# Hybrid attention encoder layer on one core: one stream of projections ahead of the attention, a shared bank for short scores, and values at odd blocks

## The chip, the cores and the metric

The kernel runs on one core of one Trainium2 chip. The metric is the device time of a run in microseconds. Engines are named TensorE (PE in the rows), VectorE (DVE), ScalarE (ACT), GpSimd (POOL) and SyncE (SP, used only to issue DMAs).

## What is computed

One encoder layer on two batches that share weights: a prompt of 1024 tokens and a sample of 512, width 1024, all in float32. Cut from the reference:

```python
hn = rms_norm(x, g_attn)
proj = hn @ w_in
qa, ka, va, qd, kd, vd = jnp.split(proj, 6, axis=-1)
oa = neighbourhood_attention(heads(qa), heads(ka), heads(va), rpb)   # 8 heads, 8 x 16 window, learned bias
od = dilated_attention(heads(qd), heads(kd), heads(vd), slopes)      # 8 heads, 3 patterns, merged by denominators
mix = jnp.concatenate([rms_norm(oa, g_na), rms_norm(od, g_dil)], axis=-1)
x = x + mix @ w_out
hn = rms_norm(x, g_ffn)
x = x + (jax.nn.silu(hn @ w_gate) * (hn @ w_up)) @ w_down
y = rms_norm(x, g_final)
```

## The kernel before

Every float32 operand of a product is split into a high and a low part, and a product is three matmuls: high by high, high by low, low by high (`mm3`, L155). Scores take two matmuls, since q holds its high part in 64 partitions and its low part in the other 64, and k's low parts stand in tiles of their own, `klow`.

**Pairs and blocks.** The 16 heads are taken two at a time, as 16 "pairs" (head pair times batch): pairs 0 to 7 of the prompt (R), 8 to 15 of the sample (S), each time dilated ("b") and neighbourhood ("a") in turn, so even pairs are dilated. A pair has 2 heads by 8 query blocks = 16 blocks in the prompt, and 8 blocks in the sample. A block goes through

- `scores`: two matmuls (L698 with k's high, L699 with k's low part) for each stretch of keys. A dilated prompt block has two stretches, a long one of 512 columns (`sc`) and a short one of 256 (`sc2`); other blocks have one;
- `softmax`: VectorE adds the bias table and takes the minimum, reading the scores' bank and writing `t` and `mt` (L739), ScalarE takes the exponential (L746);
- `turn`: transposes of `t` on TensorE (L756; 6 in a dilated prompt block, 3 in a neighbourhood one), eviction into `pT`, high part by ScalarE (L760), low part by VectorE (L761);
- `values`: matmuls of two blocks with V into one half of the bank `pv` (L776), then `head_out` on VectorE and GpSimd.

**Projections beside them.** While the blocks of pair i run, the q, k and v projections of pair i+1 are issued (`qkv`): three weight slices (v, q, k in this order) by one or two chunks of 512 tokens, in steps of six matmuls (L155, `acc<-hth,whi` and its two companions), 24 steps = 144 matmuls for a prompt pair and 72 for a sample pair. `Dense` spreads the steps evenly: block j may have consumed the share (j + 0.8)/n before its softmax and (j + 1)/n after it. After a projection's matmuls follow: for k the copies to `ka` (ScalarE) and the subtractions to `klow` (VectorE, `low(0)` and `low(1)`, L508), for v a scale, `vT` to fp16 high and low (dilated: `v16`; neighbourhood: `va`, in two halves, `v_high_a`) and transposing DMAs into `vnb` or `vna`. `after(n, f)` puts f behind n steps. Of chunk 0 of k, `low(1)` is held back (`held`) until the second-last block of the pair that runs, since `klow[1]` is a single tile that this pair's scores still read.

**What sets the order.** The engines' instruction order is made by a list scheduler from the order in which the program is written, from tile buffers and dependencies; the program's order is the priority. The opening (pair 0's projections, `opening`, with its scaling of x into hth and htl, L291 and L294) is ordered by hand on TensorE, VectorE and ScalarE. PSUM has eight banks: `mm` 2 (projections), `sc` 3 (scores), `pv` 1, `tp` 2 (transposes). Tags with their buffers in SBUF: `t` 3, `pT` 3, `p16` 3 (v16, va, dgs, bias_e), `ka` 3, `qa` 4, `tabb` 2.

**Bias tables.** `bias_load` loads the neighbourhood's relative bias into three tiles `bias_e` (nine DMAs each on SyncE, L325 and L329). `bias_rows` subtracts on VectorE (L334), writes to `e_d` in DRAM (L336), overwrites borders by GpSimd memsets (L337, L338), and writes `e2_d` (L339). It is written after pair 0's projections.

**Later phases.** After the pairs come the output projection (its first four tiles still beside pair 15) and the feed-forward (from about 830 us on), which the change doesn't touch.

Of the kernel before, what the change touches and what calls it, by code (L numbers as in the profile page):

```python
# [18 lines left out]
P = 128  # L19
# [15 lines left out]
DF = 0.8  # L35
# [3 lines left out]
TB, P16, PTB, OB = 3, 3, 3, 2  # L39
BANKS = dict(mm=("mm", 2), sc=("sc", 3), pv=("pv", 1), tp=("tp", 2))  # L40
# [16 lines left out]
def hymba_layer_kernel(  # L57
# [105 lines left out]
    def after(n, fn):  # L163
        agenda.append([n, fn])
# [8 lines left out]
    def flush():  # L173
        while agenda:
            agenda.pop(0)[1]()

    def run(gen):
        for _ in gen:
            tick()
# [37 lines left out]
    klow = [rb.tile([P, TP + 256], F32R, tag=f"kl{i}", name=f"kl{i}", bufs=1) for i in range(2)]  # L217
    held = []
# [103 lines left out]
    def bias_load():  # L322
        for t in range(3):
            f = rb.tile([P, NA + 1, 32], F32, tag="p16", name="bias_e", bufs=P16)
            nc.sync.dma_start(out=f[:, NA], in_=colm_d[t])  # L325
            for h in range(8):
                src = bass.AP(tensor=rpbf.tensor, offset=PAD + h * RPB - 4 * 31 + (-16, -8, 0)[t],
                              ap=[[1, 16], [31, NA], [1, 32]])
                nc.sync.dma_start(out=f[h * 16:(h + 1) * 16, :NA], in_=src)  # L329
            yield f  # L330
# [41 lines left out]
    def qkv(pi):  # L372
# [87 lines left out]
        def v_high_a(half):  # L460
# [10 lines left out]
            def low():  # L471
# [7 lines left out]
                if half == 0:  # L479
                    v_high_a(1)  # L480
                else:
                    v_undo()
# [11 lines left out]
        def k_put(ch, acc):  # L494
            if ch == 0:
# [5 lines left out]
                res["kl"] = [z[:, :nx] for z in klow]  # L501
# [11 lines left out]


            after(2, lambda: low(0))
            if pi and ch == 0 and st.nch == 2:
                held.append(lambda: low(1))
            else:
                after(2, lambda: low(1))
# [165 lines left out]
    def scores(k):  # L685
# [15 lines left out]
        if g == "b":  # L701
# [6 lines left out]
            if st.nch == 2:  # L708
                a, e = (1 - rr) * 512 + n * P, T + rr * P
                sc = bank("sc", "sc2")  # L710
# [188 lines left out]
    class Dense:  # L899
        def __init__(self, gen, total):  # L900
            self.gen, self.total, self.spent = gen, total, 0

        def upto(self, share):
            while self.gen is not None and self.spent < share * self.total:
                if next(self.gen, "end") == "end":
                    self.gen = None
                tick()
                self.spent += 1

        def rest(self):  # L910
            if self.gen is not None:
                run(self.gen)
            flush()

    pipe, owed = [], []

    def interleave(pi, dense):
        blocks = blocks_of(pi)
        n = len(blocks)
        tables(blocks[0])  # L920
        scores(blocks[0])
        for j, k in enumerate(blocks):
            if j + 1 < n:
                scores(blocks[j + 1])
            while j == n - 2 and held:
                held.pop()()
            dense.upto((j + DF) / n)
            softmax(k)
            pipe.append(k)
            while owed:  # L930
                head_out(owed.pop())
            if j % 2 == 0 and len(pipe) > LAG:
                values(pipe[:2])
                owed.append(pipe[1])
                del pipe[:2]
            if len(pipe) > 1:
                turn(pipe[-2])
            if j + TL < n:
                tables(blocks[j + TL])
            dense.upto((j + 1) / n)  # L940
        dense.rest()
# [4 lines left out]
    for pi in range(len(pairs)):  # L946
        if pi + 1 < len(pairs):
            dense = Dense(qkv(pi + 1), 12 * pairs[pi + 1][0].nch)
        else:
            dense = Dense(out_first(), 11 + 8 * NO)  # L950
        interleave(pi, dense)
# [505 lines left out]
```

## Time and profile before

| | us |
|---|---|
| runs | 1977.22, 1970.92, 1977.09 (median 1977.09) |
| profiled execution, its own time | 1966.33 |
| its span | 1964.3 |
| TensorE busy | 1842.0 (94%) |
| VectorE busy | 1321.1 (67%) |
| ScalarE busy | 916.4 (47%) |
| GpSimd busy | 844.1 (43%) |
| mean granted TensorE clock | 0.977 |

The rows that follow the change are of four kinds. A row of stretches gives for a window of the span the busy time of each engine with its count of instructions, the granted TensorE clock (1.00 is 2.4 GHz, the upper of its two levels; 0.5 is 1.2 GHz), and the share and rate of the DMA engines. A row of a timeline is a run of equal instructions: start, duration, engine, line, operation, tiles; in brackets the time that the engine idled before it and what ended the idling. A row of waits groups such idle time by what waited and what it waited for: total, times, longest. Rows of one line list what its instructions waited for.

### The profile page before, as it was taken

The numbers are of one execution on the slowest core, as the hardware profiler recorded it, in microseconds if no ns is written. First come the engines' busy times: TensorE is split into PE (matmuls) and PEld (weight loads), VectorE is DVE, ScalarE is ACT, GpSimd is POOL, SyncE is SP. The second block draws the span as 40 slices with busy tenths as digits, with TensorE's granted clock in tenths as the row PEclk, the third lists the DMA queues.
The fourth block names the chain that finished last, engine by engine and source line by source line (L and its number), as shares of the span: only waits on it lengthen the run. The fifth ranks groups of instructions, "written<-read, shape, count | busy, mean of one in ns | idle before, by whom it ended". The sixth has DMA issues, their size and how long they took to land.

```text
span 1964.3 us, 28970 instructions
## 1 busy us (share of the span) xinstructions
PE 1842.0 (94%) x10450; PEld 1609.9 (82%) x10450; DVE 1321.1 (67%) x2626; ACT 916.4 (47%) x1731; POOL 844.1 (43%) x690
## 2 busy tenths in 40 slices
PE   6889999898999998999899999879999997999998
PEld 4777777677777776788899999879999995877886
DVE  7566656656656567566976777877767665757765
ACT  5455557555566667443433333433333332324431
POOL 4323324232355551100666666656666543642110
PEclk9999999999899998999999999989999998999999
DMA  7623323232344455353354343334343448866642
GB/s 263 142 66 99 88 82 104 58 88 69 97 108 119 117 164 143 136 161 118 107 150 130 108 131 101 113 109 122 105 131 104 132 127 314 272 217 234 226 166 94
DMA packets 218943, 265.97 MB, mean 135 GB/s; under 512 B 59584, under 2 KB 163152, under 8 KB 218800
## 3 DMA queue, kind: packets, MB, share of 16 engines
q1 hardware_dynamic: 196176, 179.57, 30.4%
q0 software_dynamic: 22624, 84.56, 14.5%
q8 instruction: 82, 1.34, 0.3%
q14 instruction: 61, 0.50, 0.1%
HBM read 202.71 MB, written 51.41 MB: 129 GB/s over the span
## 4 chain that ended last, share of the span: by engine, by line
PE 74%; DVE 9%; DMA 7%; issue 4%; ACT 3%; POOL 2%; SPq 0%; DVEq 0%; POOLq 0%; ACTq 0%
PE acc L155 37%; PE yacc L155 11%; PE zacc L155 7%; PE mmacc L155 7%; PE pt L756 4%; PE pv L776 3%; PE sc L698 2%; DVE flo L1080 2%; PE sc L699 2%; DMA left<-hid_d 1%; DMA fraw<-in_w_up_dram 1%; POOL fs L1084 1%; DVE t L739 1%; PE pt L210 1%; DMA wq<-in_w_down_dram 1%
## 5 line engine op out<-in xcount | busy, mean ns | idle before, releaser
L155 PE MATMUL acc<-dhi,left 128*128 128x512 f32 x924 | 289.8, 394 | 16.6 <-ACT left L1254 14.0
L155 PE MATMUL acc<-hth,whi 128*128 128x512 f32 x576 | 233.5, 405 | 7.1 <-DVE kl L508 5.4
L155 PE MATMUL acc<-htl,whi 128*128 128x512 f32 x576 | 231.3, 401 | 1.0 <-POOL htl L294 0.5
L1080 DVE TENSOR_TENSOR flo<-fs,fhi 128x512 fp32r<-128x512 f32 x176 | 173.8, 991 | 86.2 <-ACT fhi L1079 85.1
L155 PE MATMUL acc<-hth,wlo 128*128 128x512 f32 x576 | 230.5, 400 | 0.1
L155 PEld LDWEIGHTS acc<-dhi,left 128*128 128x128 f32 x924 | 174.1, 189 | 57.8 <-ACT left L1254 15.3
L1079 ACT ACTIVATE fhi<-fs 128x512 fp32r<-128x512 f32 x176 | 109.5, 629 | 188.3 <-POOL fs L1084 81.4
L125 POOL TENSOR_TENSOR wlo<-wraw,whi 128x1024 fp32r<-128x1024 f32 x48 | 115.7, 2411 | 165.9 <-ACT whi L124 154.8
L155 PE MATMUL acc<-dlo,left 128*128 128x512 f32 x462 | 181.5, 393 | 0.0
L746 ACT ACTIVATE t<-t,mt 128x768 f32<-128x768 f32 (+3 forms) x192 | 138.1, 720 | 68.5 <-DVE mt L739 64.4
L760 ACT ACTIVATE pT<-pt 128x512 f16<-128x512 f32 (+2 forms) x256 | 118.8, 485 | 108.3 <-PE pt L756 107.1
L1084 POOL TENSOR_TENSOR fs<-fraw 128x512 f32<-128x512 f32 x88 | 131.6, 1510 | 83.6 <-DMA fraw<-in_w_up_dram 76.6
L1080 DVE TENSOR_TENSOR flo<-fraw,fhi 128x512 fp32r<-128x512 f32 x132 | 160.4, 1216 | 0.3 <-ACT fhi L1079 0.2
L1238 POOL TENSOR_TENSOR wq<-wq 128x512 f32<-128x512 f32 x55 | 92.3, 1689 | 156.7 <-DMA wq<-in_w_down_dram 124.5
L761 DVE SCALAR_TENSOR_TENSOR pT<-pt,pT 128x512 f16<-128x512 f32 (+2 forms) x256 | 136.8, 550 | 14.0 <-ACT pT L760 13.0
L1079 ACT ACTIVATE fhi<-fraw 128x512 fp32r<-128x512 f32 x132 | 82.9, 629 | 115.0 <-PE yacc L155 92.4
L155 PEld LDWEIGHTS acc<-hth,whi 128*128 128x128 f32 x576 | 109.9, 191 | 31.2 <-DVE kl L508 6.9
L756 PE MATMUL pt<-ident,t 128*128 128x128 f32 x768 | 125.6, 283 | 6.2 <-DVE pT L761 5.0
L1255 DVE TENSOR_TENSOR left<-left,left 128x1408 fp32r<-128x1408 f32 x42 | 74.4, 1773 | 83.8 <-ACT left L1254 83.8
L155 PEld LDWEIGHTS acc<-htl,whi 128*128 128x128 f32 x576 | 110.1, 191 | 24.9 <-DVE htl L294 2.1
L791 POOL TENSOR_TENSOR ob<-ob,den 128x256 f32<-128x256 f32 x48 | 29.6, 617 | 234.1 <-DVE ob L785 99.5
L1198 POOL TENSOR_TENSOR as<-a,as 128x384 f32<-128x384 f32 x66 | 89.0, 1348 | 91.9 <-DVE a L1187 72.5
(219 smaller groups left out, 4980.7 us busy)
## 6 DMA issues: line engine op xcount, KB each, us to landing
wq<-in_w_down_dram SPq DMA_DIRECT2D x132, 256.0 KB
hid_d<-as POOLq DMA_DIRECT2D x22, 1344.0 KB, 8.0
left<-hid_d SPq DMA_DIRECT2D x42, 704.0 KB
wraw<-in_w_in_dram POOLq DMA_DIRECT2D x46, 512.0 KB, 5.0
fraw<-in_w_gate_dram SPq DMA_DIRECT2D x45, 512.0 KB
fraw<-in_w_up_dram SPq DMA_DIRECT2D x45, 512.0 KB
tabb<-in_tabb_dram POOLq DMA_DIRECT2D x8, 800.0 KB, 4.9
xh<-x_d SPq DMA_DIRECT2D x12, 512.0 KB
```

What stands on the lines that cost most here:

```text
L125: eng.tensor_tensor(out=lo, in0=src, in1=hi.bitcast(F32), op=ALU.subtract))
L155: latest[0] = nc.tensor.matmul(out=out, lhsT=a, rhs=b, start=first and i == 0, stop=i == last, skip_group_check=not first)
L746: nc.scalar.activation(t, t, AF.Exp, bias=mt, scale=-1.0, accum_out=k.den)
L756: nc.tensor.transpose(out=pt[:, c * P:(c + 1) * P], in_=k.t[:, (c0 + c) * P:(c0 + c + 1) * P], identity=ident)
L760: nc.scalar.activation(hi, pt, AF.Copy, scale=16384.0)
L761: nc.vector.scalar_tensor_tensor(out=lo, in0=pt, scalar=16384.0, in1=hi, op0=ALU.mult, op1=ALU.subtract)
L1079: nc.scalar.activation(hi, src, AF.Copy)
L1080: nc.vector.tensor_tensor(out=lo, in0=src, in1=hi.bitcast(F32), op=ALU.subtract)
L1084: nc.gpsimd.tensor_tensor(out=o, in0=a, in1=b, op=op)
L1198: nc.gpsimd.tensor_tensor(out=part[n], in0=p, in1=q, op=op)
L1238: nc.gpsimd.tensor_tensor(out=src, in0=src, in1=other, op=q[1])
L1255: nc.vector.tensor_tensor(out=lo, in0=raw_lo, in1=hi.bitcast(F32), op=ALU.subtract)
```

## The change

- **One stream.** `Dense`, `interleave` and `held` go. `stream()` runs through the projections of all pairs and `out_first`, and `advance` takes steps from it. `target(pi, j)` says how many steps are to be spent after block j of pair pi: the even share, but of block j + 1 + LEAD, with LEAD = 2, and past a pair's end in the next pair's projections. `step(g)` handles block g of one list over all pairs: softmax, `turn` of the block before, `head_out`, at odd blocks `values` of the two oldest blocks, then the next block's scores (after the softmax; before, ahead of it), bias tables three blocks ahead across the border of pairs. A block of a new pair is scored only once its `k` is marked whole.
- **Values at odd blocks.** Before, the pairs of blocks were summed at even blocks, ahead of `turn`; now at odd ones, behind it.
- **Short scores.** `sc` has two banks instead of three, and one bank `s2` is a tile that stays: the short stretch goes to its first or second half of 256 columns, by the block's parity.
- **klow.** A third tile: `kl[1]` alternates between `klow[1]` and `klow[2]` by pair; `kl[0]` stays single. Both subtractions run two steps after the matmuls.
- **Smaller ones.** `p16` has two buffers instead of three; `bias_e` moves from `p16` to the tag `pT`; the second half of a neighbourhood pair's `va` is written three steps after the first, not at once.

```diff
-DF = 0.8
+LEAD = 2
-TB, P16, PTB, OB = 3, 3, 3, 2
-BANKS = dict(mm=("mm", 2), sc=("sc", 3), pv=("pv", 1), tp=("tp", 2))
+TB, P16, PTB, OB = 3, 2, 3, 2
+BANKS = dict(mm=("mm", 2), sc=("sc", 2), s2=("s2", 1), pv=("pv", 1), tp=("tp", 2))
-    klow = [rb.tile([P, TP + 256], F32R, tag=f"kl{i}", name=f"kl{i}", bufs=1) for i in range(2)]
-    held = []
+    klow = [rb.tile([P, TP + 256], F32R, tag=f"kl{i}", name=f"kl{i}", bufs=1) for i in range(3)]
...
-            f = rb.tile([P, NA + 1, 32], F32, tag="p16", name="bias_e", bufs=P16)
+            f = rb.tile([P, NA + 1, 32], F32, tag="pT", name="bias_e", bufs=PTB)
...
-                    v_high_a(1)
+                    after(3, lambda: v_high_a(1))
...
-                res["kl"] = [z[:, :nx] for z in klow]
+                res["kl"] = [klow[i][:, :nx] for i in (0, 1 + pi % 2)]
...
-            after(2, lambda: low(0))
-            if pi and ch == 0 and st.nch == 2:
-                held.append(lambda: low(1))
-            else:
-                after(2, lambda: low(1))
+            def lows():
+                low(0)
+                low(1)
+                if ch == st.nch - 1:
+                    res["whole"] = True
+
+            after(2, lows)
...
-                sc = bank("sc", "sc2")
+                if "s2" not in heads:
+                    heads["s2"] = bank("s2", "s2")
+                sc = heads["s2"][:, k.j % 2 * 256:k.j % 2 * 256 + 256]
...
+    totals = [12 * st.nch for st, _, _ in pairs] + [11 + 8 * NO]
+    counts = [2 * st.nq for st, _, _ in pairs]
...
+    def target(pi, j):
+
+        base, j = sum(totals[1:pi + 1]), j + 1 + LEAD
+        if pi == len(pairs) - 1:
+            return base + totals[pi + 1] * j / (counts[pi] + LEAD)
+        if j <= counts[pi]:
+            return base + totals[pi + 1] * j / counts[pi]
+        n = counts[min(pi + 1, len(pairs) - 1)] + (LEAD if pi + 2 == len(pairs) else 0)
+        return base + totals[pi + 1] + totals[pi + 2] * (j - counts[pi]) / n
...
+    def step(g):
+        k = todo[g]
+        softmax(k)
+        if pipe:
+            turn(pipe[-1])
+        pipe.append(k)
+        while owed:
+            head_out(owed.pop())
+        if k.j % 2 and len(pipe) > LAG:
+            values(pipe[:2])
+            owed.append(pipe[1])
+            del pipe[:2]
+        if g + 1 < len(todo):
+            nxt = todo[g + 1].pi
+            while not done.get(nxt, {}).get("whole"):
+                advance()
+            scores(todo[g + 1])
+        if g + TL < len(todo):
+            tables(todo[g + TL])
+        while spent[0] < target(k.pi, k.j):
+            was = spent[0]
+            advance()
+            if spent[0] == was:
+                break
```

How the order moves is shown at three places, by rows of the engines' instruction order (line, operation, output <- inputs, shape; a number in a name tells one buffer's tile from another).

On ScalarE, in the later blocks of pair 0, before: exponentials of `t`, evictions of `pt`, and one copy `vT` of a projection.

```order
L746 ACTIVATE t,den<-t,mt 128x768
L760 ACTIVATE pT<-pt 128x256
L760 ACTIVATE pT<-pt 128x512
L746 ACTIVATE t,den<-t,mt 128x768
L760 ACTIVATE pT<-pt 128x256
L760 ACTIVATE pT<-pt 128x512
L418 ACTIVATE vT<-acc 128x512
L746 ACTIVATE t,den<-t,mt 128x768
```

After, the same engine at the same blocks of pair 0:

```order
L762 ACTIVATE pT<-pt 128x256
L748 ACTIVATE t,den<-t,mt 128x768
L417 ACTIVATE vT<-acc 128x512
L762 ACTIVATE pT<-pt 128x512
L762 ACTIVATE pT<-pt 128x256
L748 ACTIVATE t,den<-t,mt 128x768
L124 ACTIVATE whi<-wraw 128x1024
L762 ACTIVATE pT<-pt 128x512
L762 ACTIVATE pT<-pt 128x256
L417 ACTIVATE vT<-acc 128x512
L748 ACTIVATE t,den<-t,mt 128x768
L441 ACTIVATE v_0_1569<-vT,vsc 128x1024
```

Both chunks of v of a later pair (`vT<-acc`) and their fp16 copy (`v_0`) have moved in between the blocks of pair 0, where before there was one chunk close to its end.

On GpSimd in the opening, before: the low parts of the second chunk (`htl`), two bias tables' loads for the dilated heads (`tabb`), and then weights.

```order
L136 DMA wraw<-in_w_in_dram 128x8x128
L294 TENSOR_TENSOR htl<-xt,hth 128x512
L679 DMA tabb<-in_tabb_dram 128x1600
L294 TENSOR_TENSOR htl<-xt,hth 128x512
L679 DMA tabb<-in_tabb_dram 128x1600
L294 TENSOR_TENSOR htl<-x_both,hth 128x512
L294 TENSOR_TENSOR htl<-xt,hth 128x512
L125 TENSOR_TENSOR wlo<-wraw,whi 128x1024 x2
```

After, on GpSimd at the same place:

```order
L293 TENSOR_TENSOR htl<-xt,hth 128x512
L679 DMA tabb<-in_tabb_dram 128x1600
L336 MEMSET bias_e 128x256
L337 MEMSET bias_e 128x224
L336 MEMSET bias_e 128x256
L337 MEMSET bias_e 128x224
L293 TENSOR_TENSOR htl<-xt,hth 128x512
L679 DMA tabb<-in_tabb_dram 128x1600
L336 MEMSET bias_e 128x256
L337 MEMSET bias_e 128x224
L293 TENSOR_TENSOR htl<-x_both,hth 128x512
L293 TENSOR_TENSOR htl<-xt,hth 128x512
```

The six memsets on the bias tables, which stood behind four weight splits and four weight loads, now stand between the low parts.

On ScalarE, at the two halves of pair 1's values (`va`), before:

```order
L468 ACTIVATE va_814<-vT,vsc 128x512 x2
L746 ACTIVATE t,den<-t,mt 128x768
L468 ACTIVATE va_887<-vT,vsc 128x512 x2
L124 ACTIVATE whi<-wraw 128x1024
L535 ACTIVATE qa_879<-acc 64x512
L535 ACTIVATE qa_880<-acc 64x512
```

After, at the same place:

```order
L467 ACTIVATE va_778<-vT,vsc 128x512 x2
L535 ACTIVATE qa_844<-acc 64x512
L535 ACTIVATE qa_845<-acc 64x512
L748 ACTIVATE t,den<-t,mt 128x768
L467 ACTIVATE va_956<-vT,vsc 128x512
L762 ACTIVATE pT<-pt 128x512
L467 ACTIVATE va_956<-vT,vsc 128x512
L762 ACTIVATE pT<-pt 128x256
L748 ACTIVATE t,den<-t,mt 128x768
L124 ACTIVATE whi<-wraw 128x1024
```

The second half has moved behind the evictions of q and an exponential, with an eviction `pT` between its two copies.

## Rows read from the trace of the kernel before

**Rows 1.** The page: span, and busy time, share and instructions of each engine.

```profile
span 1964.3 us, 28970 instructions
...
PE 1842.0 (94%) x10450; PEld 1609.9 (82%) x10450; DVE 1321.1 (67%) x2626; ACT 916.4 (47%) x1731; POOL 844.1 (43%) x690
```

**Rows 2.** Stretches of the span, all engines; the first line names the columns.

```profile
core 0: us, PE busy (x) PEld busy (x) DVE busy (x) ACT busy (x) POOL busy (x), PEclk, DMA share, GB/s
76.00:84.00 8.00, 2.39 (x9) 1.51 (x8) 2.79 (x5) 0.00 (x0) 0.00 (x0) 0.86 0.99 178
84.00:90.00 6.00, 6.00 (x32) 4.84 (x31) 3.91 (x15) 3.34 (x7) 1.06 (x4) 0.62 0.69 252
112.00:136.50 24.50, 18.50 (x170) 13.96 (x169) 18.04 (x53) 16.23 (x36) 7.94 (x9) 1.00 0.21 67
136.50:159.00 22.50, 22.50 (x150) 18.75 (x147) 11.38 (x31) 10.28 (x20) 5.94 (x6) 1.00 0.26 81
308.00:317.00 9.00, 7.04 (x70) 5.52 (x68) 8.08 (x27) 8.30 (x20) 5.00 (x5) 1.00 0.46 133
476.00:503.00 27.00, 18.25 (x128) 12.69 (x126) 21.26 (x48) 14.52 (x29) 9.52 (x15) 0.78 0.33 105
744.00:761.00 17.00, 9.13 (x52) 6.28 (x50) 12.61 (x40) 15.72 (x30) 4.02 (x6) 0.80 0.72 134
830.00:1964.00 1134.00, 1084.02 (x5609) 1001.11 (x5607) 798.01 (x1179) 422.62 (x695) 537.69 (x374) 0.98 0.47 150
```

**Rows 3.** TensorE's timeline around one dilated block where it runs densely.

```profile
94.59 0.28 PE L698 MATMUL sc<-ka,qa 128*128 128x256 f32 x1
94.71 0.28 PE L699 MATMUL sc<-kl,qa 128*128 128x256 f32 x1
94.83 0.40 PE L155 MATMUL acc<-htl,whi 128*128 128x512 f32 x1
...
95.78 0.82 PE L756 MATMUL pt<-ident,t 128*128 128x128 f32 x6
96.43 0.62 PE L776 MATMUL pv<-vnb,pT 128*128 128x64 f16 x11
96.86 0.48 PE L698 MATMUL sc<-ka,qa 128*128 128x512 f32 x1
97.17 0.39 PE L699 MATMUL sc<-kl,qa 128*128 128x512 f32 x1
97.40 0.39 PE L155 MATMUL acc<-hth,wlo 128*128 128x512 f32 x1
```

**Rows 4.** TensorE's timeline in 112 to 136.50: idle before short scores.

```profile
116.62 0.39 PE L698 MATMUL sc<-ka,qa 128*128 128x256 f32 x1 [1.62 <-DVE mt L739]
119.82 0.39 PE L698 MATMUL sc<-ka,qa 128*128 128x256 f32 x1 [0.68 <-DVE mt L739]
```

**Rows 5.** Timelines in the opening: SyncE's queue, VectorE, GpSimd, TensorE.

```profile
23.90 1.79 SPq L302 DMA_DIRECT2D xt<-in_xT_prompt_dram  x2
...
71.23 5.03 SPq L329 DMA_DIRECT2D bias_e<-in_rpbf_dram  x8
...
76.97 4.99 SPq L329 DMA_DIRECT2D bias_e<-in_rpbf_dram  x8
82.05 0.88 SPq L336 DMA_DIRECT2D e_d<-bias_e  x2
...
81.21 0.93 DVE L334 TENSOR_TENSOR bias_e<-bias_e 128x736 f32<-128x736 f32 x1 [6.45 <-DMA bias_e<-in_rpbf_dram]
...
48.20 1.30 POOL L294 TENSOR_TENSOR htl<-xt,hth 128x512 fp32r<-128x512 f32 x1 [0.75 <-ACT hth L291]
84.77 0.30 POOL L337 MEMSET bias_e<- 128x256 f32 x1 [9.60 <-DMA e_d<-bias_e]
...
50.10 0.50 PE L155 MATMUL acc<-htl,whi 128*128 128x512 f32 x1 [0.21 <-DVE htl L294]
82.80 0.58 PE L698 MATMUL sc<-ka,qa 128*128 128x256 f32 x1 [5.61 <-DVE mt L739]
```

**Rows 6.** Waits of TensorE from 60 to 1050 us: total, times, longest.

```profile
PE sc L698 <- DVE mt L739: 19.5, 23, 5.6
PE acc L155 <- DVE kl L508: 5.4, 3, 2.0
```

**Rows 7.** Line L473 (low parts of `va` on VectorE): what it waited for.

```profile
  DMA vna<-va: 12.1, 6
```

More of the change, by code (lines that the diff above doesn't have):

```diff
@@ L896, in out_first @@
             yield from out_tile(i, NO)
[L899 to L913, printed above, removed]
@@ L915, in hymba_layer_kernel @@
-    pipe, owed = [], []
[L917 to L941, printed above, removed]
+    totals = [12 * st.nch for st, _, _ in pairs] + [11 + 8 * NO]
@@ new lines, in hymba_layer_kernel, with stream, advance @@
+    counts = [2 * st.nq for st, _, _ in pairs]
+    def stream():
+        for pi in range(1, len(pairs)):
+            at[0] = pi
+            for _ in qkv(pi):
+                yield
+        at[0] = len(pairs)
+        yield from out_first()
+    at = [1]
+    dense, spent = stream(), [0]
+    def advance(n=1):
+        for _ in range(n):
+            if next(dense, "end") == "end":
+                return
+            tick()
+            spent[0] += 1
+    def target(pi, j):
[6 more added lines that the diff above has]
+        return base + totals[pi + 1] + totals[pi + 2] * (j - counts[pi]) / n
@@ new lines, in hymba_layer_kernel @@
+    pipe, owed = [], []
+    todo = [k for pi in range(len(pairs)) for k in blocks_of(pi)]
+    def step(g):
[22 more added lines that the diff above has]
+                break
@@ L945, in hymba_layer_kernel @@
     flush()
[L946 to L951, printed above, removed]
+    for k in todo[:TL]:
+        tables(k)
+    scores(todo[0])
+    for g in range(len(todo)):
+        step(g)
+    for _ in dense:
+        tick()
+    flush()
     while owed:
```

## The prediction

> **What bounds the kernel now.** The page comes first: TensorE is busy 94% of the span and no other engine is over 67% [rows 1]. Its work is not changed in amount, so the change can only touch the stretches in which TensorE idles or runs at a lower clock. The rows of stretches [rows 2] say where these are. Everything from 830 us on (feed-forward, 1134.00 us, TensorE busy 1084.02) is written alike in both kernels, so what the change can win lies in the first 830 us. There a block pair such as 136.50 to 159.00, in which projection matmuls lie between the blocks, has TensorE busy for all of its 22.50 us. Beside it stand five kinds of loss, each with a row: the end of the opening (76 to 90), a run of blocks with no projections among them (112 to 136.50), the weaker run of neighbourhood blocks (308 to 317), the chunk of the sample (476 to 503) and the wait for w_out (744 to 761). I call a block with next to no projection matmul since the block before a **free block**; I counted them in TensorE's order of both kernels.
>
> What a free block costs: a block with two score stretches issues 22 matmuls (4 scores, 6 transposes, 12 values), so the 170 of 112 to 136.50 are 7.7 blocks, 24.50 / 7.7 = 3.2 us each. Where TensorE runs densely, the starts of one such block's pieces lie 94.59 to 94.83 (short scores, 0.24), 95.78 to 96.43 (transposes, 0.65), 96.43 to 96.86 (values, 0.43) and 96.86 to 97.40 (long scores, 0.54), that is 1.9 us [rows 3]. The loss is 3.2 - 1.9 = 1.3 us per block; by idle time alone it is (24.50 - 18.50) / 7.7 = 0.8. What TensorE waits for there is mostly VectorE's pass that reads the scores (mt L739, waits of 1.62 and 0.68 us [rows 4]).
>
> **The change part by part.**
>
> *Opening, -1.5 us.* Before, the bias tables are loaded into the tag p16, whose buffers are held until the values' transposes of pair 0 are done. So VectorE's additions wait for landings until 81.21, TensorE idles 5.61 us before 82.80 [rows 5], and 84 to 90 runs at a granted clock of 0.62, which costs 6.00 x (1 - 0.62) = 2.3 [rows 2]. Together 7.9 us. After, the tables go into the tag pT, free at that time, and SyncE issues all 27 loads right behind the chunk loads that end at 23.90 + 1.79. Eight take 4.99 us, so 27 take about 17, to 43. The second table's loads had been issued by 76.26 and its addition began at 81.21, 5 us later (SyncE's row of 71.23 ends there; the third's start at 76.97 [rows 5]); so the third table is added at about 48 to 49, and its memsets wait one trip to DRAM more: 84.77 against an issue at 82.05, 2.7 us. In the new order of GpSimd the first two tables' memsets stand ahead of the second htl and the third's ahead of the last two htl. GpSimd's last htl began at 48.20; it would now begin at 48.5 + 0.9 + 2.7 + 0.6 (two memsets) + 1.3 (one htl) = 54, 5.4 to 5.8 later, and TensorE's last group of the opening (50.10) hangs on these. With half the clock's price for the new gaps (1.0) that is +6.4 against -7.9. If the landings are early, nothing of it shows: -7.9. If one more trip of 2.7 and the whole clock price lie on the way: 5.4 + 2.7 + 2.3 - 7.9 = +2.5. I take the middle of the mechanism, since before these loads met DMA engines at a share of 0.99 (76 to 84 [rows 2]).
>
> *Free blocks of the dilated prompt pairs, -5.* In pairs 0, 2, 4, 6 there are 6, 8, 6 and 10 before, since half of K's low part is held in its bank until the pair's end. With the third klow tile and the targets two blocks ahead, they are 3, 6, 6 and 11, mostly in runs of three. 4 fewer x 1.3 = -5. Ends: 0 (shorter runs lose the same in sum) and -8 (a run of three lives partly on the three buffers of t).
>
> *Free blocks of the neighbourhood pairs, +2.* They go from 9 to 15 (pairs 1, 3, 5 begin with five). 308 to 317 has 9.00 - 7.04 = 1.96 idle over 70 matmuls, at 11 per block 6.4 blocks, so 0.3 each: +2 (0 to +4).
>
> *Sample's dilated pairs 8, 10, 12, -5.* 11 free blocks become 5. No row isolates one; between 0.3 and 1.3 I take 0.8: -5 (-8 to -2).
>
> *Chunk of the sample, -4.* 476 to 503 has 27.00 - 18.25 = 8.75 idle [rows 2], because VectorE scales the chunk beside blocks and a row's bank takes one of mm's two. The steps now stand in a stretch of free blocks for five of eight slices, and beside projections for three. I take half: -4 (-8.7 to 0).
>
> *K's low parts, -3.* TensorE waits three times for kl, 5.4 us in all [rows 6]; without the held half the bank comes free two steps after its matmuls. The single klow[0] still orders one chunk of a pair behind the last use in the pair before, so not all goes: -3 (-5.4 to 0).
>
> *Values of the neighbourhood pairs, +3.* p16 has two buffers instead of three. Before, VectorE waits for the transposes of the first half, 12.1 us in six waits [rows 7], which TensorE hardly sees. After, ScalarE's copies of the second half wait for the same transposes, three steps later, with pT evictions and exponentials queued behind them on ScalarE, and TensorE waits for those. The three steps hide most of it: +3 (0 to +12.1).
>
> *At nothing.* Values beside odd blocks shift the same 12 matmuls by one block; cover is the third pT buffer, and if that fails TensorE waits for an eviction as it does in 0.68 us steps already [rows 4]. Two banks for the long scores instead of three, and scores written after the softmax, are covered where projections lie between, and are inside the bounds per free block elsewhere. The wait for w_out (744 to 761, 17.00 us with 9.13 busy [rows 2]) stays.
>
> *The short scores' bank, 0 in the sum.* Before, every score stretch turns through three banks. After, all short stretches share one bank tile, in two halves, and in the order each short score waits for VectorE's read of the previous block's short half. In dense stretches a block lasts longer than that read, so I take 0; the upper end is the 0.68 us of [rows 4] per block, which is the slower rival.
>
> The Trainium skill speaks against this part: "PSUM — Partial Sum Buffer", section "PSUM bank collisions raise a hardware error", has a TensorE write and a VectorE access kept apart by bank and quadrant even at different columns, so the two halves would not be two buffers but one. No row of before shows a shared bank for scores; [rows 4] shows what such a wait costs with separate ones.
>
> **Sum.** -1.5 - 5 + 2 - 5 - 4 - 3 + 3 = -13.5 us. The profiled execution took 1966.33 us (span 1964.3 and 2.0 around it); 1966.3 - 13.5 = 1952.8. The median of the runs, 1977.09, lies 10.8 above the profiled execution, and I carry that along: 1963.6, say **1964**. The distances to the ends, taken as independent, are about 10 below (root of 6.4², 3², 2², 3², 4.7², 2.4², 3²) and 13 above (4², 5², 2², 3², 4², 3², 9²): 1954 to 1977 for this case alone.
>
> **The rivals.**
> *More than the sum.* The bias tables land early enough (the whole 7.9 goes), and the runs of three cost half: -7.9 - 5 - 8 - 4 and the rest about -6: some -29, 1944 to 1950. For it: in the dense stretch nothing idles at all [rows 2]. Against: the DMA share of 0.99 beside such loads.
> *It doesn't do what it says.* The stream two blocks ahead only shifts the projections: what pairs 0 and 2 win, pairs 1, 3, 5 lose to their five free blocks at the start, and ScalarE's waits for the values' transposes take the upper end: -13.5 + 2 + 9 = -2.5, about 1975, 1971 to 1981. For it: the projections per pair are the same 144 matmuls, and a free block is only ever moved.
> *Slower: the shared bank.* If each of the 64 dilated prompt blocks waits the 0.68 us of [rows 4] because its short scores go out only when the previous short half has been read, that is 64 x 0.68 = 43.5, less the 13.5 already claimed: +30, 2007 at the most. With about two thirds of the blocks hit it is +16, 1993. It outweighs the sum from 13.5 / 64 = 0.21 us per block. For it: VectorE reads that half last in its block, and the wait on mt is already TensorE's largest, 19.5 us [rows 6]. Against: most of these blocks have 20 or so projection matmuls between.
>
> The Trainium skill, "Perfetto Trace Analysis", section "Optimization Strategy", reads a gap that recurs through a stretch as a sign of too few buffers; by that, p16 and sc with one buffer less each would widen the waits of [rows 4] and [rows 7]. The trace agrees that these waits recur; it doesn't show their price with fewer buffers.
>
> **How the numbers follow.** Forecast 0.48, more 0.17, no change 0.17, slower by the bank 0.18. A measurement of this kernel can tell about 0.3%, that is 6 us: faster is below 1971, slower above 1983. Faster takes most of the forecast (its own range reaches 1977; 0.39), the case of more (0.17) and a little of no change (0.03): 0.59. Slower is the bank (0.18) and tails of the others (0.03): 0.21. Between: 0.20. The range of 8 in 10 reaches from 1944 to 1988: it leaves out the outer half of the slower case and a few hundredths below.
>
> **What would show it.** The stretch after the opening: TensorE's wait for mt near 82 us gone, and GpSimd's htl at about 54 instead of 48.20 (if it stays at 48, the rival of more has its first term). The row of PE waiting for kl gone or halved. Waits of TensorE on mt: 19.5 us before; well below it with the forecast, over 40 with the slower rival, and then with the short scores as what waits. The runs of free blocks: 3.2 us per block still, but three at a time. A row of ScalarE waiting for the vna transposes, with evictions behind. What would make it wrong: a scheduling effect in the feed-forward, whose text doesn't change, or a clock that falls in the new runs as it does at 84 to 90.

## The result and the profile after

The changed kernel takes 1985.02 us (median of 6 runs) against 1974.24 before (6 runs): the ratio is 1.0057, interval 1.0034 to 1.0079. It is slower by 0.6%, where I had forecast it faster by 0.7%; the time lies in the range that I gave, on the wrong side. The profiled execution took 1982.88 us, its span is 1981.1.

The page of the changed kernel (span; busy time, share and instructions of each engine) shows the same work as [rows 1]:

```profile
span 1981.1 us, 28959 instructions
...
PE 1853.3 (94%) x10450; PEld 1617.5 (82%) x10450; DVE 1329.6 (67%) x2626; ACT 917.8 (46%) x1731; POOL 847.3 (43%) x691
```

First the question where the time went. The last transposes of pair 15 on TensorE, before and after:

```profile
806.56 0.38 PE L756 MATMUL pt<-ident,t 128*128 128x128 f32 x2
```

```profile
825.81 0.39 PE L758 MATMUL pt<-ident,t 128*128 128x128 f32 x2
```

They begin 19.3 us later; the spans differ by 16.8. So all of the loss is ahead of the feed-forward, in the opening and among the pairs. There, five stretches of the changed kernel, in the columns of [rows 2], and behind them 40 to 60 of the kernel before:

```profile
40.00:60.00 20.00, 11.40 (x35) 8.43 (x35) 14.46 (x24) 7.42 (x12) 7.74 (x12) 0.76 0.85 231
60.00:76.00 16.00, 16.00 (x63) 12.92 (x63) 8.07 (x14) 7.48 (x11) 6.79 (x4) 0.87 0.09 33
151.40:160.40 9.00, 7.39 (x68) 5.41 (x66) 7.01 (x21) 6.70 (x16) 3.81 (x4) 1.00 0.19 58
306.00:322.00 16.00, 9.25 (x55) 6.33 (x52) 6.25 (x20) 8.00 (x22) 5.16 (x8) 0.62 0.93 175
446.00:458.00 12.00, 3.84 (x36) 2.95 (x34) 5.20 (x18) 5.63 (x13) 2.50 (x4) 0.80 0.78 139
```

```profile
40.00:60.00 20.00, 19.07 (x79) 14.03 (x78) 14.37 (x24) 11.26 (x18) 9.09 (x6) 1.00 0.21 76
```

The third row is what I had looked at: a run of three free blocks, 9.00 / 3 = 3.0 us each. The other four of the changed kernel are the loss, in three places. In the opening TensorE idles 20.00 - 11.40 = 8.6 us and then runs at 0.76 and 0.87, which costs 11.40 x 0.24 + 16.00 x 0.13 = 4.8; before, the end of the opening cost 5.6 + 2.3 [rows 2, 5], and 40 to 60 another 0.9 idle (19.07 busy of 20.00). So by these stretches the opening is 4.6 worse, not 1.5 better. In pair 3 (306 to 322) 16.00 - 9.25 = 6.8 us are idle and 9.25 x 0.38 = 3.5 go to the clock. In pair 5 (446 to 458) 12.00 - 3.84 = 8.2 are idle.

Who waits for what there, by the timelines of the changed kernel. The opening, on SyncE's queue (loads and writes of the bias tables), VectorE (the subtraction on them, and the last scaling), GpSimd and TensorE:

```profile
28.07 7.07 SPq L328 DMA_DIRECT2D bias_e<-in_rpbf_dram  x8
...
50.76 0.52 SPq L335 DMA_DIRECT2D e_d<-bias_e  x1
...
38.86 0.93 DVE L333 TENSOR_TENSOR bias_e<-bias_e 128x736 f32<-128x736 f32 x1 [6.38 <-DMA bias_e<-in_rpbf_dram]
43.61 1.83 DVE L333 TENSOR_TENSOR bias_e<-bias_e 128x736 f32<-128x736 f32 x1 [0.96 <-DMA bias_e<-in_rpbf_dram]
48.41 0.92 DVE L333 TENSOR_TENSOR bias_e<-bias_e 128x736 f32<-128x736 f32 x1 [1.05 <-DMA e_d<-bias_e]
...
53.67 1.39 DVE L285 SCALAR_TENSOR_TENSOR xt<-xt,gn,row 128x512 f32<-128x512 f32 x2
...
56.50 0.31 POOL L336 MEMSET bias_e<- 128x256 f32 x1 [3.95 <-DMA taba<-e_d]
...
58.23 1.27 POOL L293 TENSOR_TENSOR htl<-xt,hth 128x512 fp32r<-128x512 f32 x1
...
42.70 0.50 PE L155 MATMUL acc<-hth,whi 128*128 128x512 f32 x1 [2.50 <-ACT hth L290]
46.09 0.79 PE L155 MATMUL acc<-htl,whi 128*128 128x512 f32 x1 [2.89 <-DVE htl L293]
...
58.31 0.80 PE L155 MATMUL acc<-htl,whi 128*128 128x512 f32 x1 [3.21 <-POOL htl L293]
```

TensorE's three waits add up to 2.50 + 2.89 + 3.21 = 8.6 us, all of its idle time in 40 to 60.

Pair 3, on ScalarE (squares of the sample's half tiles, line 258), VectorE and TensorE:

```profile
316.73 0.63 ACT L258 ACTIVATE xhalf<-xhalf 128x512 f32<-128x512 f32 x1 [4.26 <-DMA xhalf<-in_x_sample_dram]
...
317.49 0.56 DVE L741 CUSTOM_DVE_ANT_0 t<-sc,taba 128x384 f32<-128x384 f32 x1 [4.42 <-ACT xhalf L258]
...
318.11 0.69 PE L698 MATMUL sc<-ka,qa 128*128 128x384 f32 x1 [4.53 <-DVE mt L741]
```

Pair 5, on VectorE and TensorE:

```profile
455.59 0.68 DVE L272 TENSOR_SCALAR dgs<-ident,rs_x 128x128 f32<-128x128 f32 x3 [6.62 <-DMA vnb<-v]
...
456.88 0.87 PE L758 MATMUL pt<-ident,t 128*128 128x128 f32 x3 [7.64 <-DVE pT L763]
```

In each place one engine stands before an instruction of side work (a bias table, a half tile, a row of scales), and the blocks' work behind it in that engine's order starts only when that instruction has run. `dgs` waits since it takes one of p16's two buffers while both hold the dilated pair's `v16`, which DMA is transposing. In pair 3 the loads themselves also took longer: the half tiles' loads over the whole run, their size and the median from issue to landing, before and after:

```profile
xhalf<-in_x_sample_dram POOLq DMA_DIRECT2D x8, 256.0 KB, 3.1
```

```profile
xhalf<-in_x_sample_dram POOLq DMA_DIRECT2D x8, 256.0 KB, 3.9
```

The DMA engines' share was 0.93 in 306 to 322, against 0.54 in 277 to 303 of the kernel before, where these loads ran then. No run parts this from the wait for buffers of `t`.

The waits of TensorE that answer to [rows 6], from 60 to 1050 us, and from 218 to 600 the wait of short scores on the shared bank:

```profile
PE sc L698 <- DVE mt L741: 15.0, 21, 4.5
PE pt L758 <- DVE pT L763: 11.9, 17, 7.6
...
PE acc L155 <- DVE kl L507: 4.1, 7, 0.9
...
PE s L698 <- DVE mt L741: 0.2, 1, 0.2
```

### The profile page after: what moved, and what is told of

The parts are those of the page before. It is cut to its first block, busy times and chain, and to the rows that moved or that the text cites. A ratio compares the mean times of both kernels' runs of the same rounds, so it can differ in the third digit from the quotient of the medians.

```text
span 1981.1 us, 28959 instructions
## 1 busy us (share of the span) xinstructions
PE 1853.3 (94%) x10450; PEld 1617.5 (82%) x10450; DVE 1329.6 (67%) x2626; ACT 917.8 (46%) x1731; POOL 847.3 (43%) x691
## 4 chain that ended last, share of the span: by engine, by line
PE 65%; DMA 9%; DVE 8%; POOL 5%; issue 5%; ACT 3%; SPq 0%; DVEq 0%; POOLq 0%; ACTq 0%
PE acc L155 35%; PE yacc L155 9%; PE zacc L155 6%; PE mmacc L155 6%; PE pt L758 3%; DVE flo L1102 3%; DMA wq<-in_w_down_dram 2%; PE pv L778 2%; DMA fraw<-in_w_up_dram 2%; POOL fs L1106 2%; POOL wq L1260 2%; PE sc L698 2%; PE sc L699 1%; POOL as L1220 1%; DMA left<-hid_d 1%
## 5 line engine op out<-in xcount | busy, mean ns | idle before, releaser
L155 PEld LDWEIGHTS acc<-hth,wlo 128*128 128x128 f32 x576 | 111.5, 194 | 23.6 <-POOL wlo L125 0.9
```

What stands on the lines that cost most here:

```text
L155: latest[0] = nc.tensor.matmul(out=out, lhsT=a, rhs=b, start=first and i == 0, stop=i == last, skip_group_check=not first)
```

## The experiments

Theory after the result: three pieces of side work cost what the stream wins (bias tables, dgs, the sample's sums). Rival: the stream or the shared bank costs by itself. Every run stood beside runs of the kernel before on its chip; I compare by the ratio to those, and 0.001 is 2.0 us. The intervals are 0.0013 to 0.0023 on either side, so that a difference of two ratios is good to about 0.003, or 6 us. Traces are of one execution each, and its time can lie several us from the median.

**e1_bias: the subtraction behind the opening.**

```diff
-            nc.vector.tensor_tensor(out=f[:, :NA], ...
+            add = nc.vector.tensor_tensor(out=f[:, :NA], ...
+            tc.add_manual_dep(add.ins, heads["mark"].ins.name, ...
...
             follow(b, [proj(2, 1), proj(0, 1)], [[], [], [], []])
+            heads["mark"] = latest[0]
```

> The changed kernel, with one edit: VectorE's subtraction on the bias tables additionally waits for the last projection matmul of the opening that needs a low part of the second chunk; the loads stay where they are. Theory (three side users of buffers and queues cost the time, not the stream): VectorE's 6.38 us wait before the first subtraction and the memsets between GpSimd's low parts go, GpSimd's last low part is back at about 48 instead of 58.23, TensorE's first dilated block ends at about 73 instead of 86.8, and the time falls by 8 to 13 us, since the tables are also ready before the first scores that need them. Rival (the opening is bound by the DMA queues that the early loads fill): the last low part stays behind 54, gain below 4 us.

1974.22 us, ratio 0.9994 (0.9978 to 1.0010): 0.0063 below the changed kernel, 12 us. VectorE's subtractions and GpSimd's last low part in this run, two stretches of it, and 40 to 90 of the changed kernel and of the kernel before:

```profile
53.50 2.59 DVE L333 TENSOR_TENSOR bias_e<-bias_e 128x736 f32<-128x736 f32 x3
...
47.92 1.29 POOL L293 TENSOR_TENSOR htl<-xt,hth 128x512 fp32r<-128x512 f32 x1 [0.74 <-ACT hth L290]
...
40.00:60.00 20.00, 19.27 (x81) 14.47 (x80) 15.84 (x26) 10.95 (x17) 8.89 (x6) 1.00 0.75 174
40.00:90.00 50.00, 49.23 (x242) 38.84 (x241) 34.41 (x71) 27.52 (x45) 20.92 (x19) 1.00 0.83 179
```

```profile
40.00:90.00 50.00, 41.40 (x163) 32.84 (x163) 29.44 (x58) 21.79 (x35) 21.83 (x20) 0.86 0.62 149
```

```profile
40.00:90.00 50.00, 43.46 (x192) 33.69 (x191) 27.63 (x59) 21.56 (x37) 19.58 (x16) 0.93 0.62 145
```

The low part is back at 47.92, and TensorE is busy and at a granted clock of 1.00 in both stretches of this run. By 40 to 90 the opening loses 50.00 - 49.23 = 0.8 us here, 8.6 + 41.40 x 0.14 = 14.4 in the changed kernel and 6.5 + 43.46 x 0.07 = 9.6 before. So the 12 us are the changed kernel's excess and, beyond it, most of what the opening had lost before. The loads are the same early ones, so it was the instructions that wait for them, not the queues. The theory holds.

**e2_dgs: dgs from pT.**

```diff
-rb.tile([P, 512], F32, tag="p16", name="dgs", bufs=P16)
+rb.tile([P, 512], F32, tag="pT", name="dgs", bufs=PTB)
```

> The changed kernel, with one edit: the tile dgs (the row of scales for a chunk) takes its buffer from the tag pT instead of p16. Theory: VectorE's wait of 6.62 us for the transposes of the dilated values in pair 5 (which hold both buffers of p16) goes, with TensorE's 7.64 us behind it: 6 to 8 us less. Rival (pair 5's free blocks lose it anyway, since scores, values and exponentials run at the pace of VectorE there): less than 3 us.

1977.77 us, ratio 1.0021 (1.0005 to 1.0038): 0.0036 or 7 us below the changed kernel, and VectorE has no wait before dgs any more. The theory holds.

**e3_sums: the sample's sums nine steps later.**

```diff
-            extra, by_chunk = sample_sums(), False
+            def sums():
+                for _ in range(9):
+                    yield
+                yield from sample_sums()
+            extra, by_chunk = sums(), False
```

> The changed kernel, with one edit: the sums of squares of the sample (eight half tiles in the tag t, loaded by GpSimd's queue) begin nine projection steps later. Theory: in the changed kernel they fall on pair 3's five free blocks, where ScalarE waits 4.26 us for a load and the scores behind it for their buffer of t; beside projections this is hidden, and pair 3 loses about 5 us instead of 15.4: 8 to 11 us less. Rival (the same waits appear wherever the half tiles are): less than 3 us.

1984.35 us, ratio 1.0052 (1.0033 to 1.0072): 1 us, nothing that this comparison can tell, and less than the 8 us forecast. The wait has moved with the half tiles, now to blocks beside projections; ScalarE, VectorE and TensorE of this run, and 300 to 345 in this run and in the changed kernel:

```profile
320.17 0.63 ACT L258 ACTIVATE xhalf<-xhalf 128x512 f32<-128x512 f32 x1 [3.54 <-DMA xhalf<-in_x_sample_dram]
...
326.77 0.56 DVE L745 CUSTOM_DVE_ANT_0 t<-sc,taba 128x384 f32<-128x384 f32 x1 [7.36 <-ACT xhalf L258]
...
327.39 0.44 PE L702 MATMUL sc<-ka,qa 128*128 128x384 f32 x1 [1.78 <-DVE mt L745]
```

```profile
300.00:345.00 45.00, 39.18 (x240) 30.61 (x239) 24.54 (x66) 27.56 (x66) 17.75 (x21) 0.89 0.51 107
```

```profile
300.00:345.00 45.00, 35.45 (x208) 27.60 (x207) 24.58 (x74) 24.62 (x62) 14.51 (x18) 0.81 0.43 93
```

VectorE waits longer than before the edit, but TensorE, with projections to do, waits 1.78 us where it had waited 4.53. In this stretch the run loses 5.8 + 39.18 x 0.11 = 10.1 us and the changed kernel 9.6 + 35.45 x 0.19 = 16.3. So the edit does part of what the theory says, 6 us in pair 3, and the whole time doesn't show it: the two profiled spans, 1980.0 and 1981.1, differ by 1 us. Where the rest goes is not shown. By these rows free blocks make the half tiles dearer for pair 3, but that does not settle the time.

**e4_three: all three edits.** The diff is the three above together.

> The three edits at once: subtraction behind the opening, dgs from pT, sample sums nine steps later. Theory: the gains add, 22 to 32 us below the changed kernel and 10 to 20 below the kernel before, so about 1955 to 1963. Rival (the stream two blocks ahead costs by itself): not below the kernel before.

1964.48 us, ratio 0.9946 (0.9925 to 0.9967): 22 us below the changed kernel and 10.7 below the kernel before. The gains add up (12 + 7 + 1 = 20). The rival falls: with the side work out of its way, the change is faster than before.

**f1_before_bias: the kernel before with the bias edit alone.** bias_e in pT, and the dependency of e1_bias.

> The kernel before, with one edit: the bias tables are loaded into the tag pT (so early, as in the changed kernel) and VectorE's subtraction waits for the opening's last projection that needs a low part. No stream, no shared bank, no third klow. Theory (what the three repairs left of the change is mostly this): TensorE's 5.61 us before 82.80 and the half clock behind it go, 7 to 9 us less than before, about 1965 to 1967, so that the stream, the shared bank and the klow tile together are worth within 4 us of the run with the three edits (1964.5). Rival (the stream itself wins what I forecast for it, some 12 us): this run stays near before, 1970 or more, or the run with three edits lies 8 us or more below it.

1967.54 us, ratio 0.9993 (0.9976 to 1.0010): nothing, and 9 us above e4_three. The rival holds: the stream, the tile and the banks are worth some 9 us together, and the opening alone is worth nothing in the kernel before. TensorE's waits for K's low parts in this run, from 85 to 830 us, show one place to which the gain goes:

```profile
PE acc L155 <- DVE kl L510: 15.4, 5, 4.5
```

Before it was 5.4 [rows 6]: when the blocks start earlier, the held half of K is what stands in the way. The opening itself is repaired in this run:

```profile
40.00:90.00 50.00, 49.01 (x228) 38.13 (x227) 34.02 (x70) 28.92 (x48) 20.11 (x19) 1.00 0.80 176
```

It loses 1.0 us there instead of 9.6, and 10.0 come back as the wait for kl. The profiled execution took 1978.30, the longest of this kernel's twelve, so the rows show where it waits rather than how long a usual execution takes.

**f2_three_sc3: short scores back in the ring of three.**

```diff
-sc=("sc", 2), s2=("s2", 1)
+sc=("sc", 3)
-                sc = heads["s2"][:, k.j % 2 * 256:k.j % 2 * 256 + 256]
+                sc = bank("sc", "sc2")
```

> The changed kernel with the three edits, and with the short scores back in the ring of three score banks (no s2). Theory: the shared bank costs nothing, since TensorE waited 0.2 us in all before short scores for VectorE's read of the other half; within 4 us of 1964.5. Rival (my slower case: the shared bank holds short scores back): 8 us or more below 1964.5.

1964.63 us, ratio 0.9976 (0.9959 to 0.9992), 0.0030 or 6 us above e4_three. It is a little beyond what the theory allowed, on the side opposite to the rival: the shared bank costs nothing that shows, and may win some 6 us, which is just what this comparison can tell.

**f3_sums_first: the sums in pair 1's first steps.** e1's and e2's edits, and `SQ = 1` for `SQ = 4`.

> The changed kernel with the repairs of the bias tables and of dgs, and with the sample's sums of squares moved to the first steps of pair 1's projections, in which no block yet uses the tag t. Theory (the half tiles cost because each holds one of t's three buffers from its load to its square, some 5 us, wherever blocks need t): pair 3 loses about 5.5 like pair 1, and the time is 8 to 10 us below the run with three edits (1964.5), about 1955. Rival (ScalarE's wait for the loads costs anywhere): 1962 or more.

1961.49 us, ratio 0.9959 (0.9944 to 0.9975), 0.0013 above e4_three, no difference. The loads now meet the end of the opening. From 60 to 90 us in this run, and in e4_three:

```profile
60.00:90.00 30.00, 26.96 (x130) 21.88 (x130) 17.43 (x41) 15.77 (x29) 15.16 (x18) 0.94 0.89 214
```

```profile
60.00:90.00 30.00, 29.93 (x163) 24.36 (x162) 18.58 (x47) 16.54 (x29) 12.00 (x14) 1.00 0.85 182
```

And from 300 to 345, likewise:

```profile
300.00:345.00 45.00, 42.58 (x280) 34.11 (x279) 31.82 (x84) 26.99 (x63) 19.14 (x21) 1.00 0.39 87
```

```profile
300.00:345.00 45.00, 39.92 (x222) 31.25 (x221) 23.17 (x64) 25.04 (x61) 16.33 (x20) 0.92 0.48 109
```

Pair 3 loses 2.4 us instead of 5.1 + 39.92 x 0.08 = 8.3, a gain of 5.9. In 60 to 90, with 33 matmuls fewer, 3.0 + 26.96 x 0.06 = 4.7 are lost instead of 0.1: what pair 3 gains is paid there. The rival holds; the half tiles cost wherever they stood in these runs.

**f4_ka4: a fourth ka buffer, one klow tile a pair.** On top of e4_three:

```diff
-    klow = [... for i in range(3)]
-    for i, z in enumerate(klow):
-        nc.gpsimd.memset(z[slice(0, 64) if i else slice(64, 128)].bitcast(F32), 0.0)
+    klow = [... for i in range(2)]
...
-                res["kl"] = [klow[i][:, :nx] for i in (0, 1 + pi % 2)]
+                res["kl"] = [klow[pi % 2][:, :nx]] * 2
...
-... tag="ka", name=f"ka{i}", bufs=3) ...
+... tag="ka", name=f"ka{i}", bufs=4) ...
```

> The changed kernel with the three edits, a fourth ka buffer, and one klow tile for both heads of a pair in turn between two tiles (each head's low part keeps its own 64 partitions; the other head's low part then meets q's low part, a product of two low parts). So a pair's K leaves its two projection banks without waiting for the pair that runs. Theory A (the five free blocks at the start of pairs 1, 3, 5 come from K sitting in both projection banks): these runs go and 8 us or more are won against 1964.5. Theory B (a free block is only moved, since the order issues projections as early as buffers allow and then has none left): the runs turn up later in the same pairs, and the time is within 5 us of 1964.5.

1949.89 us, ratio 0.9900 (0.9887 to 0.9913): 9 us below e4_three and 20 below the kernel before. Theory A by its time, though 9 us good to about 5 is close to its limit. By where the free blocks stand it is theory B: pairs 1, 3 and 5 no longer begin with five, but runs turn up later, and pair 4 has eight in a row, in the first row below. They cost less. The row after it is this run's own dense stretch.

```profile
371.00:389.30 18.30, 18.18 (x180) 14.22 (x179) 17.50 (x54) 15.55 (x34) 7.97 (x9) 1.00 0.29 89
112.00:136.50 24.50, 24.50 (x169) 20.21 (x168) 11.90 (x35) 11.27 (x21) 4.09 (x4) 1.00 0.13 39
```

180 / 22 = 8.2 blocks in 18.30 us, 2.2 us each, with TensorE idle for 0.1 us, where [rows 2] had 3.2 and the changed kernel 3.0. Which of the edits brings this is not shown.

**g1_one_klow: the tile without the fourth buffer.** f4_ka4 with ka at three.

> The run with three edits, plus one klow tile for both heads of a pair, in turn between two tiles (as in the run with four ka buffers), but ka with its three buffers. It parts the 14 us of that run. Theory A (the single klow[0] held K in the projection banks): most of the gain is here, 1953 or less. Theory B (the third ka buffer held it, since the second head's K finds no ka buffer until the running pair is done with its first head): 1960 or more, and pairs 1, 3, 5 still begin with five free blocks.

1976.41 us, ratio 1.0005 (0.9991 to 1.0019). Theory B: pairs 1, 3, 5 begin with five or six free blocks as before, and the gain of f4_ka4 hangs on the fourth ka buffer. That it is 12 us above e4_three I had not expected. One part shows in pair 4, where VectorE stands before a neighbourhood pair's low part with a score behind it, and TensorE behind that:

```profile
358.29 2.30 DVE L472 SCALAR_TENSOR_TENSOR va<-vT,vsc,va 128x512 f16<-128x512 f32 x1 [4.47 <-DMA vna<-va]
...
361.04 0.38 PE L703 MATMUL s<-ka,qa 128*128 128x256 f32 x1 [2.51 <-DVE mt L746]
```

That explains a quarter at most. The two profiled spans, 1973.5 here and 1968.5 in e4_three, differ by 5 us only, so the traces can't show the rest, and I leave it open.

**g2_p16_three: p16 with three buffers again.** On g1_one_klow, dgs back in p16 and `P16 = 3`.

> As the run with one klow tile in turn, but dgs back in p16 and p16 with three buffers, for which the saved tile makes room. Theory (p16 with two buffers cost the time through dgs alone): within 4 us of the run with one klow tile, and no wait of VectorE before dgs. Rival (two buffers also cost at the neighbourhood pairs' values, as I had forecast, some 3 us or up to 12): 4 to 12 us below it.

1968.70 us, ratio 0.9975 (0.9958 to 0.9993), 0.0030 or 6 us below g1_one_klow. The rival: on this base, beyond dgs, the missing buffer costs some 6 us; the run is still 6 us above e4_three. ScalarE's waits for the neighbourhood values' transposes, the row that I had asked for, are there in g1_one_klow (the row below) and not in this run, in which ScalarE waits 6.7 us for the dilated values' transposes instead:

```profile
ACT va L467 <- DMA vna<-va: 9.7, 5, 4.6
```

**g3_lead_zero: LEAD = 0.** On e4_three.

> The run with three edits, with LEAD = 0 instead of 2: the stream may be spent only up to the block's own share. Theory (the buffers of ka and klow, not the target, set how far the projections run ahead): the free blocks at the start of pairs 1, 3, 5 are six instead of five, and the time is within 5 us of 1964.5. Rival (two blocks of lead are what the stream wins): 8 us or more above it.

1974.63 us, ratio 0.9998 (0.9984 to 1.0013), 0.0052 or 10 us above e4_three. The runs of free blocks in pairs 1, 3, 5 are six, as expected, but the time is not: the theory falls, the two blocks of lead are worth about 10 us.

**g4_spaced_sums: f4_ka4 with the sums at every second step.**

```diff
-                for _ in range(9):
-                    yield
-                yield from sample_sums()
+                for _ in sample_sums():
+                    yield
+                    yield
```

> The run with four ka buffers (1949.9), with the sample's sums of squares at every second projection step from the first on, instead of nine steps late and at every step. Theory (the half tiles cost because they come close together and hold t's buffers in turn): pair 3 loses some 2 us less, 1946 to 1950. Rival (their loads cost anywhere): 1950 to 1954.

1950.70 us, ratio 0.9880 (0.9867 to 0.9894), 0.0020 below f4_ka4, less than this comparison can tell, so that neither the theory nor the rival is decided. It is the fastest of the runs by its ratio: 1.2% below the kernel before and 1.8% below the changed one.

## Why the prediction was wrong

**The stream came near its terms.** Without the opening the terms of my sum are -12; with the opening repaired in both kernels, e4_three lies 9 us below f1_before_bias. That e4_three is 10.7 below the kernel before, near the sum of -13.5, is in part luck: its opening is repaired as well, for which the sum had only -1.5. Of the single terms few were measured. A run of three free blocks costs 3.0 us per block, near the 3.2 of the kernel before. The neighbourhood pairs begin with five free blocks. The lead is worth 10 us (g3_lead_zero). The term for K's low parts, -3, did not come: the wait for kl went from 5.4 to 4.1 us in the changed kernel and is 7.0 in e4_three, in nine waits. The sum of the rival of more is a slip: -7.9 - 5 - 8 - 4 - 6 is -31, not -29; its range of 1944 to 1950 holds either.

**The opening is the first step that failed.** I took -1.5, from -7.9 to +2.5; it was +4.6 by the stretches. I had priced one wait, the third table's on GpSimd, from the landing of its loads. The third subtraction came when I had said, at 48.41. But the scaling that feeds every later low part stands in VectorE's order behind each of the three subtractions, which wait 6.38 + 0.96 + 1.05 us, so that the last scaling ends at 55.06 and TensorE waits at three places, not one. GpSimd's trip to DRAM comes on top: from the end of the third subtraction (49.33) to its memset (56.50) it is 7.2 us, where I had put 2.7. So the last low part began at 58.23 and not at 54. I had put the mechanism down for GpSimd and left it out for the engine ahead of it. The first table's landing alone, 3.7 us after its last load was issued (35.14 to 38.86), would have given the 6 us, since VectorE's row of scales is done at 32.5. e1_bias shows what a right order wins: 12 us against the changed kernel, that is the 4.6 and about the 7.9 that the rival of more had for the opening. And f1_before_bias shows that this 7.9 was no gain by itself in the kernel before: it came back as the wait for kl.

**p16 is the second.** Its term was +3, with +12.1 as the end, from the neighbourhood values. Measured it is 7, through dgs alone (e2_dgs); on the base of g1_one_klow a third buffer is worth 6 more (g2_p16_three), and whether the two add up in the changed kernel no run shows. I costed the user of the tag that the diff touches and not the others. The row of scales `dgs` is allocated beside running blocks only once, in the sample's chunk (its other rows stand in the opening), and it was there that both buffers were taken. The stretch that I had down for -4 (the sample's chunk) is where the loss was. The edit that I let pass as cleared by three steps did show as ScalarE's wait, 5.9 us in the changed kernel.

**The sample's sums are the third, shown by their waits alone.** They have no term in my sum. Before, they ran from 277 to 303 beside projections, with TensorE busy throughout:

```profile
277.00:303.00 26.00, 26.00 (x162) 20.95 (x161) 14.26 (x39) 19.25 (x46) 12.42 (x14) 1.00 0.54 156
```

With the stream, five of the eight loads are issued within 8 us (305.3 to 313.0), and each half tile holds one of the three buffers of t from its load to its square. Pair 3 has 10.3 us of loss in 306 to 322. Both places that I tried instead took some 6 us off pair 3 and gave them back elsewhere (e3_sums, f3_sums_first): what is shown is the wait, not that the whole time would be shorter without it.

**The slower rival was wrong.** I gave it 0.18 with the shared bank as its mechanism. Short scores waited 0.2 us in all for VectorE's read of the other half, and the ring of three did no better (f2_three_sc3). The Trainium skill has a TensorE write and a VectorE access to one bank kept apart even at different columns ("PSUM — Partial Sum Buffer", section "PSUM bank collisions raise a hardware error"). The trace agrees: no matmul of a short score overlaps a read of that bank, and the keeping apart cost no more than the 0.2 us. What buffers were worth stood elsewhere: a fourth ka buffer 21 us (g1_one_klow against f4_ka4), a third p16 buffer 6 on the same base. The Trainium skill takes a gap that recurs as a possible sign of too few buffers ("Perfetto Trace Analysis", section "Optimization Strategy"). For ka and p16 these runs agree; the costliest wait of the changed kernel for want of a buffer, that of dgs, was a single one.

**What stays open.** Why g1_one_klow is 12 us above e4_three, beyond the 2.5 us shown; where the 6 us go that e3_sums wins in pair 3; and by which place the lead wins its 10 us, since the runs of free blocks hardly differ.

## What to carry to other kernels

When a change moves or cuts a tag's buffers, list every tile of the tag and not only those in the diff; the one that is allocated once can be the one that finds no room. When loads are moved up, what matters is where the instruction that waits for them stands on its in-order engine, and all such waits have to be counted, on each engine in turn. A stall that is taken away can come back at the next wait, as in f1_before_bias, so the idle time of a stretch is not yet a gain. And how far a stream may run ahead hangs on its target and on its rings of buffers: here the fourth ka buffer was worth 21 us, the target's two blocks 10.

## What I had not expected of the hardware

The price of a free block was no limit of an engine here. In the kernel before, VectorE was busy 18.04 of 24.50 us in such a run [rows 2], and TensorE idled 6.0; in f4_ka4, with about the same work per block in another order, TensorE idles 0.1 of 18.30 and VectorE is busy 17.50 (96%). The long stalls of TensorE went with a lower clock: the granted clock was 0.62 over 306 to 322, where TensorE was busy 9.25 of 16.00 us, and 1.00 over 371 to 389 in f4_ka4, where it was busy throughout. Idle time in short pieces did not always: 112 to 136.50 of the kernel before has 6.0 us of it at 1.00 [rows 2].
